# First half of the first norm's row spread over the partitions by TensorE, with identity products before and after it

## The chip, the cores and the metric

The kernel runs on one core of a Trainium2 chip. The metric is the device time of one execution in microseconds (us), taken as the median of several runs. Each profile shown here belongs to one execution, which has its own time. Times in the views count from the start of the profiled span.

Engines are named as in the profile: PE is the matrix engine (TensorE), PEld its weight load, DVE the vector engine, ACT the scalar engine, POOL the general engine (GpSimd), SP the engine that here does nothing but issue transfers (DMAs).

## The reference

One layer of a hybrid decoder block on 512 tokens of width 2048. What the change touches is only the very first step: the norm of the input and the projection behind it.

```python
def rmsnorm(x, g):
    xf = x.astype(jnp.float32)
    y = xf * lax.rsqrt(jnp.mean(xf * xf, axis=-1, keepdims=True) + EPS)
    return (y * g.astype(jnp.float32)).astype(x.dtype)
...
h = rmsnorm(x, attn_pre_norm[l])
m = token_mixer(h, w_in[l], ...)
x = x + rmsnorm(m, attn_post_norm[l])
h = rmsnorm(x, ffn_pre_norm[l])
f = conv_ffn(h, w_ffn_in[l], conv_w[l], conv_b[l], w_ffn_out[l])
x = x + rmsnorm(f, ffn_post_norm[l])
```

The gain `g` of the first norm, `attn_pre_norm`, is a row of 2048 numbers. Every token, that is every partition of a tile, needs the same row.

## The kernel before

Tokens stand in four tiles of 128 (t = 0 to 3), the width in 16 slots of 128. All matrix products are made in three passes: each float32 operand is split into a high part, rounded by ACT (`act(hi, raw, AF.Copy)`, L122, or L135 for activations), and a low remainder by DVE (`tt(lo, raw, hi, subtract)`, L123, or L136). PE then multiplies hi by hi, hi by lo and lo by hi (L176 to L178, L158 to L160, and later in the program L909 to L911 and L1006 to L1008). A weight block of 512 KB (`raw`, four buffers) becomes one pair `whi`, `wlo`.

`first_half` opens the program. It normalizes the tokens and makes the first half of one projection while the data still arrives. For each token tile t:

- `load_x(t)` fetches the tile in two transfers of 512 KB each (`xt`), and `load_w` fetches weight blocks.
- `bcast_row` fetches half of the gain row with one transfer that writes the same 4 KB to all 128 partitions of `gb` (512 KB written). The first half of the row is fetched right behind tile 0, the second at the end.
- `square(t)` sums squares on ACT (L231, in two halves), POOL forms the inverse root (L233, L129, L131: the tile `rs`).
- `scale(t, i)` multiplies on DVE by `rs` and by quarter i of `gb` (L238, 128x512 each).
- `turn(t, i)` transposes four 128x128 blocks on PE against the identity `ident` (L143), and splits the result into `ah` (ACT, L135) and `al` (DVE, L136).
- `prods(t, g)` makes the six products of token tile t with weight block g (L176 to L178).

The order in which PE, ACT, DVE and POOL run the steps of `first_half` is the order in which the code is written. SP isn't among these engines: where its transfers stand in its queue is chosen by the scheduler, from a simulated time line. The same scheduler orders all engines in the rest of the program. All transfers of SP use eight completion counters in turn (`DMAHW0` to `DMAHW7`), so SP issues a transfer only when the one issued eight places before it has landed. That makes SP's queue readable: when a transfer is issued late, the one eight places ahead has just landed.

Far behind, at the end of the feed-forward part, `down_unit` (L1006 to L1008) starts when the pool `ff` takes over the memory of an earlier pool. Every fourth weight block there is split into `xhi`, `xlo` of that pool in place of `whi`, `wlo`.

`bank()` gives a PSUM bank from a ring of four (pool `psa`), `qk_tile` a 128x512 tile from a ring of six.

Of the kernel before, what the change touches and what calls it, by code (L numbers as in the profile page):

```python
# [9 lines left out]
F32 = mybir.dt.float32  # L10
# [7 lines left out]
P = 128  # L18
# [17 lines left out]
def hybrid_layer(ctx: ExitStack, tc: tile.TileContext, x, attn_pre_norm, w_in, w_alpha_up, b_alpha,  # L36
# [3 lines left out]
    nc = tc.nc  # L40
# [6 lines left out]
    def dma(o, i):  # L47
        return nc.sync.dma_start(out=o, in_=i)
# [7 lines left out]
    mm = nc.tensor.matmul  # L56
# [3 lines left out]
    few = ctx.enter_context(tc.tile_pool(name="few", bufs=1, side="right"))  # L60
# [4 lines left out]
    ident = few.tile([P, P], F32, name="ident")  # L65
# [11 lines left out]
    def bank(pool=None):  # L77
        return (pool or psa).tile([P, 512], F32, name="bank", tag="bank")
# [21 lines left out]
    def load(src, a):  # L100
        raw = wpool.tile([P, GR], F32, name="raw", tag="raw", bufs=4)
        dma(raw.rearrange("p (a b) -> p a b", a=a), src)
        return raw
# [8 lines left out]
    def granule(src, a, raw=None, spare=None, bufs=4, hl=None):  # L112
        if raw is None:
            raw = load(src, a)
        if hl is not None:
            hi, lo = hl[:, 0, :], hl[:, 1, :]
        elif spare:
            hi = spare.tile([P, GR], F32R, name="xhi", tag="xhi", bufs=bufs)
            lo = spare.tile([P, GR], F32R, name="xlo", tag="xlo", bufs=bufs)
        else:  # L120
            hi, lo = halves()
        act(hi, raw, AF.Copy)  # L122
        tt(lo, raw, hi.bitcast(F32), ALU.subtract)  # L123
        r = "p (a b) -> p a b"
        return hi.rearrange(r, a=a), lo.rearrange(r, a=a)

    def rsqrt_mean(ss, n, width=1):
        t = small.tile([P, width], F32, name="ms", tag="ms")
        nc.gpsimd.tensor_scalar(t, ss, 1.0 / n, EPS, ALU.mult, ALU.add)  # L129
        r = small.tile([P, width], F32, name="rs", tag="rs")  # L130
        nc.gpsimd.tensor_tensor(r, t, nhalf[:, :width], ALU.pow)  # L131
        return r
# [5 lines left out]
    def transpose_into_act(src, t, slot0, n):  # L138
        for g in range(0, n, 4):
            m = min(4, n - g)  # L140
            b = bank()
            for j in range(m):
                nc.tensor.transpose(b[:, j * P:(j + 1) * P], src[:, (g + j) * P:(g + j + 1) * P], ident)  # L143
            bv = b[:, :m * P].rearrange("p (k c) -> p k c", k=m)
            split(ah[:, t, slot0 + g:slot0 + g + m, :], al[:, t, slot0 + g:slot0 + g + m, :], bv)

    def bcast_row(tile_ap, row):
        dma(tile_ap, row.partition_broadcast(P))
# [23 lines left out]
    def mm_n(banks, t, g, w):  # L172
        for k in range(2):
            s = 2 * g + k
            st, sp = s == 0, s == KT - 1
            mm(banks[t], ah[:, t, s, :], w[0][:, k, :], start=st, stop=False)  # L176
            mm(banks[t], ah[:, t, s, :], w[1][:, k, :], start=False, stop=False)  # L177
            mm(banks[t], al[:, t, s, :], w[0][:, k, :], start=False, stop=sp)  # L178
# [17 lines left out]
    def big8(name):  # L196
        return mx.tile([P, 2048], F32, name=name, tag="big8", bufs=6)

    def qk_tile(name):
        return mx.tile([P, S], F32, name=name, tag="qk", bufs=6)  # L200
# [5 lines left out]
    def first_half(c):  # L206
        gb = big8("gb")
        jb = mx.tile([P, 1024], F32, name="jb", tag="jb", bufs=1)
        xts = [big8("xt") for _ in range(NT)]
        w3 = mx.tile([P, 2, GR], F32R, name="w3", tag="big8", bufs=6)  # L210
        H2 = [slice(1024 * i, 1024 * (i + 1)) for i in range(2)]
        H4 = [slice(512 * i, 512 * (i + 1)) for i in range(4)]
        rs, raws, w = {}, {}, {}
        banks = [bank(psm) for _ in range(NT)]
        col = C_GV + 512 * c

        def load_x(t):
            for i in range(2):
                dma(xts[t][:, H2[i]], x2[t * P:(t + 1) * P, H2[i]])

        def load_w(*gs):
            for g in gs:
                raws[g] = load(w_in3[:, 2 * g:2 * g + 2, col:col + 512], 2)

        def weights(g):
            w[g] = granule(None, 2, raws[g], hl=w3 if g == 3 else None)

        def square(t):
            ss = small.tile([P, 2], F32, name="ss2", tag="ss2", bufs=4)
            for i in range(2):  # L230
                act(jb, xts[t][:, H2[i]], AF.Square, accum_out=ss[:, i:i + 1])  # L231
            sm = small.tile([P, 1], F32, name="ss", tag="ss")
            nc.gpsimd.tensor_tensor(sm, ss[:, 0:1], ss[:, 1:2], ALU.add)  # L233
            rs[t] = rsqrt_mean(sm, D)

        def scale(t, *ps):
            for i in ps:
                stt(xts[t][:, H4[i]], xts[t][:, H4[i]], rs[t], gb[:, H4[i]], ALU.mult, ALU.mult)  # L238

        def turn(t, *ps):  # L240
            for i in ps:
                transpose_into_act(xts[t][:, H4[i]], t, 4 * i, 4)

        def prods(t, *gs):
            for g in gs:
                mm_n(banks, t, g, w[g])

        load_x(0)
        bcast_row(gb[:, H2[0]], attn_pre_norm[0, H2[0]])
        load_w(0, 1, 2)  # L250
        load_x(1)
        load_w(3)
        load_x(2)
        load_x(3)
        bcast_row(gb[:, H2[1]], attn_pre_norm[0, H2[1]])
        square(0)
        scale(0, 0, 1)
        weights(0)
        turn(0, 0, 1)
        weights(1)  # L260
        weights(2)
        square(1)
        prods(0, 0, 1)
        scale(1, 0, 1)
        prods(0, 2)
        weights(3)
        turn(1, 0, 1)
        square(2)
        prods(0, 3)
        square(3)  # L270
        scale(2, 0, 1)
        prods(1, 0, 1, 2)
        turn(2, 0, 1)
        prods(1, 3)
        scale(3, 0, 1)
        prods(2, 0, 1)
        turn(3, 0, 1)
        scale(0, 2, 3)
        prods(2, 2)
        turn(0, 2, 3)  # L280
        scale(1, 2, 3)
        prods(2, 3)
        turn(1, 2, 3)
        scale(2, 2, 3)
        prods(3, 0, 1)
        turn(2, 2, 3)
        scale(3, 2, 3)
        prods(3, 2)
        turn(3, 2, 3)
        prods(3, 3)  # L290
        return banks

    with tc.manual_schedule(engines=IN_ORDER):
        banks = first_half(0)
# [914 lines left out]
```

## Time and profile before

| | us |
|---|---|
| runs: median (lowest to highest of 3) | 2176.3 (2173.17 to 2177.24) |
| the profiled execution, its own time | 2167.47 |
| its span, first to last instruction | 2165.8 |
| PE busy in the span | 2127.6 |
| DVE, ACT, POOL busy | 1416.9, 900.0, 205.1 |
| mean granted TensorE clock | 0.996 of full speed |
| data moved | 303.83 MB, 140 GB/s on the mean |

A row of the time line gives start, duration, engine, line, operation and shapes, how many were merged, and in brackets how long the engine had been idle and what ended that. The chain of waits goes back from the end of a stretch: at each step to what released the work. A row of the stretches gives, for each engine, busy time and number of instructions, then the granted TensorE clock, the share of busy DMA engines and the rate in GB/s. A merged duration of matrix products overlaps: the step from one start to the next is the pace.

### The profile page before, as it was taken

What the parts mean: (1) busy time and instruction counts of PE and PEld (TensorE: products, weight loads), DVE (VectorE), ACT (ScalarE), POOL (GpSimd) and SP (SyncE); (2) the same over time, 40 slices, a digit from 0 to 9 for tenths busy, and PEclk for the clock granted to TensorE, in tenths of its full rate; (3) what the DMA queues carried; (4) which work ended last, traced back from release to release, by engine and by line L of the source; (5) the groups of instructions that cost most, each with busy time, mean ns of one, the idle gap of its engine ahead of it and who ended that gap; (6) DMA issues with size and microseconds to landing.
All of it is one profiled execution on the core that took longest, in us unless ns stands there. A gap on an engine that the chain in (4) does not pass through costs nothing.

```text
span 2165.8 us, 31887 instructions
## 1 busy us (share of the span) xinstructions
PE 2127.6 (98%) x13009; PEld 1895.7 (88%) x13009; DVE 1416.9 (65%) x1722; ACT 900.0 (42%) x1162; POOL 205.1 (9%) x245
## 2 busy tenths in 40 slices
PE   7999999999999999999999999999999899999997
PEld 6878888888888889899999999999999778888886
DVE  5345553444444236787777686787877777888987
ACT  4233332333333234344444543544444465443533
POOL 1000000000000000011101111111111011011101
PEclk9999999999999999999999999999999999999999
DMA  6322222222224334355666757667577578677663
GB/s 212 104 69 78 79 75 81 70 78 86 78 88 166 100 133 174 128 127 140 159 160 160 158 141 180 157 139 188 142 169 180 163 218 214 179 191 180 160 171 136
DMA packets 218471, 303.83 MB, mean 140 GB/s; under 512 B 11776, under 2 KB 155572, under 8 KB 216404
## 3 DMA queue, kind: packets, MB, share of 16 engines
q1 hardware_dynamic: 165204, 238.87, 32.9%
q0 software_dynamic: 53120, 62.92, 18.9%
q8 instruction: 102, 1.67, 0.3%
q14 instruction: 45, 0.37, 0.0%
HBM read 273.97 MB, written 27.79 MB: 139 GB/s over the span
## 4 chain that ended last, share of the span: by engine, by line
issue 46%; PE 45%; POOL 4%; DVE 2%; DMA 1%; ACT 1%; POOLq 0%; SPq 0%; DVEq 0%; ACTq 0%
PE bank L177 6%; PE bank L176 6%; PE bank L178 6%; PE bank L160 5%; PE bank L158 5%; PE bank L159 5%; PE bank L1007 2%; PE bank L1008 2%; PE bank L1006 2%; POOL rt L858 2%; POOL raw L858 2%; PE bank L426 1%; PE bank L494 1%; PE bank L525 1%; PE bank L143 1%
## 5 line engine op out<-in xcount | busy, mean ns | idle before, releaser
L123 DVE TENSOR_TENSOR wlo<-raw,whi 128x1024 fp32r<-128x1024 f32 x307 | 374.2, 1222 | 361.6 <-ACT whi L122 353.5
L122 ACT ACTIVATE whi<-raw 128x1024 fp32r<-128x1024 f32 x307 | 324.8, 1059 | 599.7 <-PE bank L178 158.0
L911 PE MATMUL bank<-ah,wlo 128*128 128x256 f32 x1280 | 358.1, 280 | 0.9 <-DVE wlo L123 0.9
L909 PE MATMUL bank<-ah,whi 128*128 128x256 f32 x1280 | 357.9, 280 | 0.1
L910 PE MATMUL bank<-al,whi 128*128 128x256 f32 x1280 | 357.8, 280 | 0.0
L123 DVE TENSOR_TENSOR wlo<-rt,whi 128x1024 fp32r<-128x1024 f32 x220 | 267.7, 1221 | 95.1 <-ACT whi L122 93.0
L122 ACT ACTIVATE whi<-rt 128x1024 fp32r<-128x1024 f32 x220 | 232.1, 1059 | 231.2 <-PE bank L910 169.6
L910 PEld LDWEIGHTS bank<-al,whi 128*128 128x128 f32 x1280 | 244.0, 191 | 0.1
L911 PEld LDWEIGHTS bank<-ah,wlo 128*128 128x128 f32 x1280 | 240.2, 188 | 1.4 <-DVE wlo L123 1.3
L909 PEld LDWEIGHTS bank<-ah,whi 128*128 128x128 f32 x1280 | 240.3, 188 | 0.4 <-ACT whi L122 0.3
L176 PE MATMUL bank<-whi,ah 128*128 128x512 f32 x600 | 236.6, 397 | 0.4 <-ACT ah L135 0.4
L177 PE MATMUL bank<-wlo,ah 128*128 128x512 f32 x600 | 235.6, 393 | 0.0
L178 PE MATMUL bank<-whi,al 128*128 128x512 f32 x600 | 234.9, 393 | 0.0
L158 PE MATMUL bank<-ah,whi 128*128 128x512 f32 (+1 forms) x512 | 196.0, 383 | 0.0
L160 PE MATMUL bank<-ah,wlo 128*128 128x512 f32 (+1 forms) x512 | 194.6, 380 | 0.0
L159 PE MATMUL bank<-al,whi 128*128 128x512 f32 (+1 forms) x512 | 194.4, 380 | 0.0
L1007 PE MATMUL bank<-wlo,ah 128*128 128x512 f32 x420 | 163.7, 390 | 2.4 <-DVE wlo L123 2.4
L1008 PE MATMUL bank<-whi,al 128*128 128x512 f32 x420 | 163.3, 389 | 0.0
L1006 PE MATMUL bank<-whi,ah 128*128 128x512 f32 x420 | 155.9, 390 | 0.2 <-DVE acc L1014 0.2
L178 PEld LDWEIGHTS bank<-whi,al 128*128 128x128 f32 x600 | 113.1, 188 | 24.0 <-DVE al L136 0.3
L176 PEld LDWEIGHTS bank<-whi,ah 128*128 128x128 f32 x600 | 113.1, 189 | 23.8 <-ACT ah L135 0.8
L177 PEld LDWEIGHTS bank<-wlo,ah 128*128 128x128 f32 x600 | 113.1, 189 | 23.7 <-DVE wlo L123 0.5
(259 smaller groups left out, 4084.1 us busy)
## 6 DMA issues: line engine op xcount, KB each, us to landing
raw<-in_w_in_dram SPq DMA_DIRECT2D x96, 512.0 KB, 3.7
raw<-in_w_ffn_in_dram SPq DMA_DIRECT2D x96, 512.0 KB, 4.7
raw<-in_w_ffn_out_dram SPq DMA_DIRECT2D x48, 512.0 KB, 6.3
rt<-in_w_ffn_in_dram SPq DMA_DIRECT2D x40, 512.0 KB, 5.9
rt<-in_w_ffn_in_dram POOLq DMA_DIRECT2D x40, 512.0 KB, 6.1
raw<-in_w_ffn_in_dram POOLq DMA_DIRECT2D x40, 512.0 KB, 7.4
raw<-in_w_o_dram SPq DMA_DIRECT2D x32, 512.0 KB, 3.7
rt<-in_w_ffn_out_dram SPq DMA_DIRECT2D x20, 512.0 KB, 7.7
```

The source lines that it names most:

```text
L122: act(hi, raw, AF.Copy)
L123: tt(lo, raw, hi.bitcast(F32), ALU.subtract)
L158: mm(o, wh, ah[:, t0:t1, kk, :], start=st, stop=False)
L159: mm(o, wh, al[:, t0:t1, kk, :], start=False, stop=False)
L160: mm(o, wl, ah[:, t0:t1, kk, :], start=False, stop=sp)
L176: mm(banks[t], ah[:, t, s, :], w[0][:, k, :], start=st, stop=False)
L177: mm(banks[t], ah[:, t, s, :], w[1][:, k, :], start=False, stop=False)
L178: mm(banks[t], al[:, t, s, :], w[0][:, k, :], start=False, stop=sp)
L909: mm(o, wh, sh[:, :, kk, :], start=start and kk == 0 and n == 0, stop=False, **NOW)
L910: mm(o, wh, sl[:, :, kk, :], start=False, stop=False, **NOW)
L911: mm(o, wl, sh[:, :, kk, :], start=False, stop=kk == HK - 1, **NOW)
L1007: mm(b[j], sh[:, o:o + P], w[1][:, q, :], start=False, stop=False, **NOW)
```

## The change

```diff
+        row = qk_tile("row"), qk_tile("row")
+        for i in range(2):
+            dma(row[i][0:1, :], attn_pre_norm[0:1, H4[i]])
+        ones = few.tile([1, P], F32, name="ones")
+        nc.vector.memset(ones, 1.0)
         load_x(0)
-        bcast_row(gb[:, H2[0]], attn_pre_norm[0, H2[0]])
         load_w(0, 1, 2)
+
+        def idle_products(n):
+            scratch = bank()
+            for i in range(n):
+                mm(scratch[:, :P], ident, ident, start=True, stop=True)
+
+        idle_products(3)
+        for i in range(2):
+            g = bank()
+            mm(g, ones, row[i][0:1, :], start=True, stop=True)
+            nc.vector.tensor_copy(gb[:, H4[i]], g)
+        idle_products(6)
         load_x(1)
         load_w(3)
         load_x(2)
```

The first half of the gain row is no longer written to 128 partitions by one transfer. Two transfers of 2 KB bring it to one partition, as two quarters. PE multiplies a column of 128 ones by each quarter, which puts the quarter into all 128 rows of a PSUM bank, and DVE copies the bank to `gb`. Three products of the identity with itself stand ahead of these two products on PE, six behind them; nothing reads their result. The second half of the row still comes by its broadcast transfer.

The new steps take four banks of the ring of four and two tiles of the ring of six. Lines behind the change stand 18 lines further down.

On PE, at the start of the program, the rows are these now (the transposes of L143 stood first before). A name in brackets is a counter of the engine that is waited for.

```order
L261 MATMUL bank<-ident 128x128 [waits Pool_49]
L261 MATMUL bank<-ident 128x128 x2
L266 MATMUL bank<-row,ones 128x512 [waits DMAHW0_49,DVE_49]
L266 MATMUL bank<-row,ones 128x512 [waits DMAHW1_49]
L261 MATMUL bank<-ident 128x128 x6
L143 MATMUL bank<-ident,xt 128x128 [waits DMAHW2_49,DVE_49,PE_49]
```

Eleven products stand ahead of the first transpose, the first of them behind POOL, which makes the identity, and the row's two behind their transfers.

SP's queue at the start of the program, before (the rows of `xt` come in the order of the tiles, two for each):

```order
L48 DMA xt<-in_x_dram 128x1024 x2
L48 DMA gb<-in_attn_pre_norm_dram 128x1024
L48 DMA raw<-in_w_in_dram 128x2x512 x3
L48 DMA xt<-in_x_dram 128x1024 x2
L48 DMA raw<-in_w_in_dram 128x2x512 [waits DMAHW0_49]
L48 DMA xt<-in_x_dram 128x1024 [waits DMAHW1_49]
L48 DMA xt<-in_x_dram 128x1024 [waits DMAHW2_49]
L48 DMA xt<-in_x_dram 128x1024 [waits DMAHW3_49]
L48 DMA xt<-in_x_dram 128x1024 [waits DMAHW4_49]
L48 DMA gb<-in_attn_pre_norm_dram 128x1024 [waits DMAHW5_49]
L48 DMA gnb<-in_gla_norm_dram 128x256 [waits DMAHW6_49]
L48 DMA dnb<-in_diff_norm_dram 128x256 [waits DMAHW7_49]
```

And now:

```order
L48 DMA row<-in_attn_pre_norm_dram 1x512 x2
L48 DMA xt<-in_x_dram 128x1024 x2
L48 DMA raw<-in_w_in_dram 128x2x512 x4
L48 DMA gb<-in_attn_pre_norm_dram 128x1024 [waits DMAHW0_49]
L48 DMA gnb<-in_gla_norm_dram 128x256 [waits DMAHW1_49]
L48 DMA xt<-in_x_dram 128x1024 [waits DMAHW2_49]
L48 DMA xt<-in_x_dram 128x1024 [waits DMAHW3_49]
L48 DMA xt<-in_x_dram 128x1024 [waits DMAHW4_49]
L48 DMA xt<-in_x_dram 128x1024 [waits DMAHW5_49]
L48 DMA xt<-in_x_dram 128x1024 [waits DMAHW6_49]
L48 DMA xt<-in_x_dram 128x1024 [waits DMAHW7_49]
L48 DMA dnb<-in_diff_norm_dram 128x256 [waits DMAHW0_49]
```

More has moved than the diff says. The fourth weight block, the second half of the gain row and the row `gnb`, which stood behind tile 1, now stand ahead of it. Before, tile 1 stood behind tile 0, one broadcast and three weight blocks.

One place on PE differs far from the change, in `down_unit`, where the scheduler has drawn another order (the rest of PE's program reads alike). Before:

```order
L1006 MATMUL bank<-whi,ah 128x512 x2
L1007 MATMUL bank<-wlo,ah 128x512
L1008 MATMUL bank<-whi,al 128x512
L1006 MATMUL bank<-whi,ah 128x512
L1007 MATMUL bank<-wlo,ah 128x512
L1008 MATMUL bank<-whi,al 128x512
L1007 MATMUL bank<-wlo,ah 128x512
L1008 MATMUL bank<-whi,al 128x512
L1006 MATMUL bank<-whi,ah 128x512
L1007 MATMUL bank<-wlo,ah 128x512
L1008 MATMUL bank<-whi,al 128x512
L1006 MATMUL bank<-xhi,ah 128x512 x2
```

And now (L1024 to L1026 are L1006 to L1008 of before):

```order
L1025 MATMUL bank<-wlo,ah 128x512
L1026 MATMUL bank<-whi,al 128x512
L1024 MATMUL bank<-whi,ah 128x512
L1025 MATMUL bank<-wlo,ah 128x512
L1026 MATMUL bank<-whi,al 128x512
L1025 MATMUL bank<-wlo,ah 128x512
L1026 MATMUL bank<-whi,al 128x512
L1024 MATMUL bank<-whi,ah 128x512
L1025 MATMUL bank<-wlo,ah 128x512
L1026 MATMUL bank<-whi,al 128x512
L1024 MATMUL bank<-xhi,ah 128x512 x2
L1024 MATMUL bank<-whi,ah 128x512
```

The two products that led the group now stand behind the two that read `xhi`.

## Prediction

> **What bounds the kernel now.** First the page's head, then the waits of PE over the whole span.
>
> ```profile
> span 2165.8 us, 31887 instructions
> PE 2127.6 (98%) x13009; PEld 1895.7 (88%) x13009; DVE 1416.9 (65%) x1722; ACT 900.0 (42%) x1162; POOL 205.1 (9%) x245
> ```
> ```profile
> PE bank L143 <- DVE xt L238: 10.4, 2, 9.5
> PE bank L1006 <- ACT xhi L122: 8.7, 2, 7.4
> ```
>
> PE is without work for only 2165.8 - 2127.6 = 38.2 us. One gap of 9.5 us lies at the start, where the change is, one of 7.4 us far behind. So PE sets the end, and whatever moves its start moves the end, unless a later wait takes it up. The later waits end when ACT or DVE have worked on what PE itself delivered, or when a transfer lands whose buffer PE's own progress freed, so they move along with PE. I pass a shift at the start through one to one.
>
> Next the chain of waits over the first 26 us: what released what until PE ran on without a break.
>
> ```profile
> 4.30 11.02 DMA xt<-in_x_dram
> ...
> 15.40 1.16 ACT jb L231 x2
> ...
> 17.18 0.57 POOL rs L131
> ...
> 18.45 0.74 DVE xt L238
> 19.19 1.15 DVE w L123
> ...
> 20.38 0.50 PE bank L177
> 20.88 0.23 PE bank L178
> ```
>
> This decides the case. The chain doesn't go through tile 0 and its gain row at all. It goes through the transfer of tile 1's second half, issued at 4.30 and waited for until 15.40, then its squares, its inverse root, its scaling, the split of weight block 3, and PE at 20.38. From there PE runs at a pace of 0.23 us. The time line of the transfer queue shows why tile 1 is late.
>
> ```profile
> 0.80 0.86 SPq L48 DMA_DIRECT2D xt<-in_x_dram  x2
> 1.71 0.42 SPq L48 DMA_DIRECT2D gb<-in_attn_pre_norm_dram  x1
> ...
> 3.78 0.99 SPq L48 DMA_DIRECT2D xt<-in_x_dram  x2
> ...
> 14.05 0.33 SPq L48 DMA_DIRECT2D gnb<-in_gla_norm_dram  x1
> 15.33 0.33 SPq L48 DMA_DIRECT2D dnb<-in_diff_norm_dram  x1
> ```
>
> `gnb` and `dnb` wait for the transfers eight places ahead, which are the halves of tile 1: they landed at about 14.05 and 15.33, behind all that was issued before them.
>
> **The change part by part.** First tile 0. Its steps on ACT, POOL, DVE and PE, from the time line:
>
> ```profile
> 5.66 1.06 ACT L231 ACTIVATE jb<-xt 128x1024 f32<-128x1024 f32 x1 [0.38 <-DMA xt<-in_x_dram]
> ...
> 7.45 0.56 POOL L131 TENSOR_TENSOR rs<-ms,nhalf 128x1 f32<-128x1 f32 x1
> 8.69 1.41 DVE L238 SCALAR_TENSOR_TENSOR xt<-xt,rs,gb 128x512 f32<-128x512 f32 x2 [7.03 <-DMA gb<-in_attn_pre_norm_dram]
> 9.50 1.97 PE L143 MATMUL bank<-ident,xt 128*128 128x128 f32 x8 [9.50 <-DVE xt L238]
> ...
> 17.78 1.41 DVE L238 SCALAR_TENSOR_TENSOR xt<-xt,rs,gb 128x512 f32<-128x512 f32 x2 [1.71 <-POOL rs L131]
> ```
>
> The removed broadcast held the scaling until 8.69. The inverse root was ready at 7.45 + 0.56 = 8.01, and for tile 1 DVE starts 0.04 behind it (17.18 + 0.57 = 17.75, 17.78), so without the broadcast 8.05 would do: 0.64 us to be had. Against it stand the two row transfers, issued ahead of tile 0. Two issues take 0.86 us, with the gap 0.9, so tile 0 is issued 0.9 us later and its root comes at up to 8.9. Its second half no longer shares the queue with the broadcast, which gives a little back. I take 8.9 for the scaling, 0.2 later than now (bounds 8.4 and 9.1).
>
> The new work on PE and DVE has to fit ahead of that. The identity's last step, and a plain float32 product of 512 columns for the price:
>
> ```profile
> 1.57 0.28 POOL masks.py:199 TENSOR_SCALAR_AFFINE_SELECT ident<-ident 128x128 f32<-128x128 f32 x1
> ```
> ```profile
> L382 PE MATMUL bank<-gaT,wup 80*128 80x512 f32 x8 | 3.8, 592 | 0.0
> ```
>
> PE can begin at 1.85. A 128x128 float32 product at the start costs 1.97 / 8 = 0.25 us by the eight transposes, so three cost 0.75 and six 1.5. A 512-column one costs 0.59 us at full pace, about 1.1 at the start's pace (the ratio of 0.43 to 0.23, below). Rows of 2 KB should land well before the 4.1 us at which the first 512 KB of tile 0 had. Taking 3.0: products until 5.2, the two copies on DVE (at most the 0.7 us of a scaling each) until 5.9, the six identity products until 6.7. Even with rows as late as 5.66 all is over by 9.4, while the transposes then start at 9.7. So I cost all eleven products and both copies at nothing; the wait for tile 0 hides them. Were it gone, they would cost up to 0.75 + 2.2 + 1.5 = 4.5 us.
>
> Now the term that counts, tile 1. Ahead of and with its second half, the queue moved eight transfers of 512 KB. Now it moves nine and `gnb` with 128 KB, since weight block 3, the second broadcast and `gnb` have been drawn ahead. The rates, from the stretches of the start:
>
> ```profile
> 3.00:4.50 1.50, 0.00 (x0) 0.00 (x0) 0.00 (x0) 0.37 (x1) 0.00 (x0) 1.00 0.89 309
> 4.50:6.00 1.50, 0.00 (x0) 0.00 (x0) 0.00 (x0) 1.12 (x3) 0.00 (x0) 1.00 1.00 259
> 6.00:8.00 2.00, 0.00 (x0) 0.00 (x0) 0.00 (x0) 0.81 (x2) 0.94 (x3) 1.00 0.99 261
> ...
> 9.00:12.00 3.00, 2.09 (x9) 1.69 (x9) 2.22 (x4) 1.72 (x3) 0.00 (x0) 1.00 1.05 412
> ```
>
> 640 KB more at 412 GB/s is 0.655 / 0.412 = 1.6 us. The later issue adds 0.9. On the other side, from 4.5 to 8, when the removed broadcast was under way, the queue moved only 260 GB/s at full business: 3.5 x (1 - 260 / 412) = 1.3 us lost, which may go away with it. Upper end: the broadcast that now stands in the way is as slow in its new place, 1.6 + 0.9 = +2.5. Lower end: the slowness goes, and the rows use time in which nothing moved anyway, 1.6 - 1.3 = +0.3. I take the later issue whole, since the queue is empty until then, and most of the relief: 1.6 + 0.9 - 1.1 = **+1.4 us**. It passes whole along the chain above: behind 15.40 every step waits for the one before. Weight block 3 comes earlier now, but its split stands behind tile 1's scaling on DVE.
>
> Last, the other place on PE. There the time line has:
>
> ```profile
> 1755.06 1.06 ACT L122 ACTIVATE xhi<-raw 128x1024 fp32r<-128x1024 f32 x1 [7.26 <-DMA raw<-in_w_ffn_out_dram]
> ...
> 1756.16 0.73 PE L1006 MATMUL bank<-xhi,ah 128*128 128x512 f32 x2 [1.31 <-ACT xhi L122]
> ```
>
> PE already waits 1.31 us for `xhi` here. Two products that ran ahead of the wait now run behind it, so it grows by 2 x 0.23 = 0.45 us if the transfer lands when it did, by nothing if it moves. I take **+0.2**.
>
> Sum: 1.4 + 0.2 = **+1.6 us**; tile 0's 0.2 vanishes behind tile 1. For the profiled execution (span 2165.8, 2167.47 with what lies around it) that gives 2169.1. The median of the runs stands 8.8 us above that execution; nothing in the change bears on that distance, so I forecast 2176.3 + 1.6 = **2177.9**.
>
> **The rivals.** First the clock, which could make it slower. Two starts, and stretches at the start and around the late gap:
>
> ```profile
> 15.13 0.63 PE L176 MATMUL bank<-whi,ah 128*128 128x512 f32 x1
> ...
> 15.56 0.63 PE L177 MATMUL bank<-wlo,ah 128*128 128x512 f32 x1
> ```
> ```profile
> 9.50:12.90 3.40, 2.99 (x10) 1.00 1.05 416
> 12.90:16.30 3.40, 3.40 (x8) 1.00 1.01 394
> ```
> ```profile
> 1729.80:1733.30 3.50, 0.04 (x1) 0.04 (x1) 0.06 (x1) 2.03 (x3) 0.00 (x0) 0.50 0.36 146
> 1733.30:1736.60 3.30, 3.26 (x7) 2.16 (x8) 2.39 (x2) 0.78 (x1) 0.00 (x0) 0.50 0.97 397
> ```
>
> From its first work at 9.50 to about 16.3 PE steps by 0.43 us, then by 0.23 (the granted clock of 1.00 in these rows isn't recorded for the start). After 12.9 it had no gap, from 9.5 to 12.9 only 2.99 of 3.40 were busy. In the late gap the clock reads 0.50, and stays so for 3.3 us after work returns. If now PE does tile 0's products in pieces and waits for tile 1 at about 20, the slow pace can reach beyond that wait. Each slow microsecond there loses 1 - 0.23 / 0.43 = 0.47 us. A stretch of 3.4 us loses 1.6, one as long as the first (6.8) loses 3.2: in all +3.2 to +4.8, **2180.3**. For it: three weight splits on DVE still break up tile 0's products. Against it: at the slow pace those 18 products alone fill 7.7 us nearly without a gap. It leaves no-change from a slow stretch of 5.9 us on.
>
> Second, faster: the new products bring PE to its fast pace before tile 0, and tile 1 isn't late, because transfers overlap more than I count. Eight transposes take 1.03 us at the fast pace:
>
> ```profile
> 25.73 1.03 PE L143 MATMUL bank<-ident,xt 128*128 128x128 f32 x8
> ```
>
> Then tile 0's transposes give 1.97 - 1.03 = 0.94 and the wait for the broadcast 0.64, less the 0.9 of the later issue: -0.7, with the other place -0.5, **2175.8**. For it: about 4.5 us of products stand where PE was idle. Against it: tile 1's second half would have to land at 14.6, with 640 KB more ahead of it. The most that a fast start could ever give is 6.8 x 0.47 + 0.64 = 3.8 us, below what can be told from no change.
>
> The Trainium skill, "TensorE: Matmul & The Clock Gate", section "What's actually happening", has the clock rise after about 3.4 us of sustained work and fall after one idle window of that length, with windows that run freely. By that rule the new products may lift it before tile 0, and a wait below 3.4 us mostly wouldn't drop it, which speaks for the second rival's pace and against the first. The trace agrees in the gap at 1726 to 1733, where the clock halves and comes back in steps of this size; that 2.99 busy of 3.40 didn't lift it says that small holes count.
>
> That the products don't fill the wait for tile 0 (they end near 6.7 by my sum, PE then idles 3 us) is a way in which the change wouldn't do what it says; it gives the forecast's time, as tile 1 decides.
>
> **How the numbers follow.** Forecast 0.55, slow clock 0.25, faster start 0.14, something else 0.06 (the gap of 7.4 us with its slow stretch may fall differently). The runs shown lie within 2173.17 to 2177.24, so about 0.2%, or 4.35 us, is what a measurement can tell from no change. Slower by more (above 2180.65): 0.07 from the forecast with its upper end, 0.14 from the clock, 0.03 from the rest, 0.24. Faster by more (below 2171.95): only by scatter, 0.07. Within: 0.69. The forecast's own range is 2176.6 to 2179.3 by the bounds of its terms (+0.3 to 2.5 + 0.45); with the rivals and the scatter of 2 us the range is 2173.5 to 2182.0.
>
> **What would show it.** Right: tile 1's second half lands at 16 to 17.5; ACT waits for it ahead of the second squares; PE stands idle ahead of tile 1's transposes for 1 us or more, and the unbroken run starts near 21.8. The identity products end before tile 0's scaling. Wrong: tile 1 lands by 15.3, or the pace after its transposes is 0.43, or a new wait of PE appears behind 25 us that the profile of before doesn't have.

## The result and the profile after

The change made the kernel slower, and the time lies outside the predicted range.

| | before | after |
|---|---|---|
| runs: median (lowest to highest of 5 each) | 2176.3 (2173.17 to 2182.4) | 2184.02 (2182.74 to 2185.03) |
| ratio, 95% interval | | 1.0031 (1.0016 to 1.0046) |
| profiled execution, its own time | 2167.47 | 2185.03 |
| its span | 2165.8 | 2183.3 |
| PE busy in the span | 2127.6 | 2147.7 |

The two profiled executions differ by 17.6 us, the medians by 7.7. The difference in PE's busy time, 20.1 us, is larger still although the change adds only eleven products (8.4 us by the rows below). Most of what is left over has another cause than the start, which the experiments brought out (below); the start is read first. The page's head and PE's waits of after:

```profile
span 2183.3 us, 31937 instructions
PE 2147.7 (98%) x13031; PEld 1910.3 (87%) x13031; DVE 1419.8 (65%) x1725; ACT 900.4 (41%) x1162; POOL 205.0 (9%) x245
```
```profile
PE bank L1024 <- ACT xhi L122: 8.1, 3, 7.3
PE bank L143 <- DVE xt L238: 3.9, 1, 3.9
...
PE bank L261 <- POOL ident masks.py:199: 1.9, 1, 1.9
```

The wait of 9.5 us ahead of tile 0's transposes is gone, since the new products fill it:

```profile
1.91 1.65 PE L261 MATMUL bank<-ident 128*128 128x128 f32 x6 [1.91 <-POOL ident masks.py:199]
...
3.49 3.78 PE L266 MATMUL bank<-row,ones 1*128 1x512 f32 x4
...
7.20 2.93 PE L261 MATMUL bank<-ident 128*128 128x128 f32 x12
```

Each of these products is recorded as two passes (x6 for three products, x4 for two, x12 for six). A wait of 3.9 us ahead of tile 1's transposes has come. The chain of waits over the first 28 us of after (start, duration, what):

```profile
6.30 11.85 DMA xt<-in_x_dram
...
18.23 1.16 ACT jb L231 x2
...
20.02 0.57 POOL rs L131
...
20.61 0.77 DVE xt L238
...
21.42 1.97 PE bank L143 x8
23.38 0.43 PE bank L176
...
26.79 0.31 PE bank L178
27.10 0.23 PE bank L176
```

The same chain as before decides: tile 1's second half, squares, root, scaling, and now the transposes where the split of weight block 3 came last before. Two things are new in it. The half is waited for until 18.15, and its squares start at 18.23, not 15.40. And behind the transposes PE steps by 0.43 us until 26.8. Stretches of after (PE's busy time first, the granted clock third from the end):

```profile
2.00:8.00 6.00, 6.00 (x13) 3.23 (x14) 1.38 (x2) 2.37 (x5) 0.74 (x3) 1.00 0.91 291
8.00:18.20 10.20, 9.04 (x36) 7.09 (x35) 6.64 (x8) 5.29 (x7) 0.64 (x2) 1.00 1.01 369
...
18.00:21.00 3.00, 0.00 (x0) 0.00 (x0) 0.39 (x1) 2.24 (x5) 0.94 (x3) 0.83 1.03 423
...
20.00:24.00 4.00, 2.58 (x10) 2.42 (x11) 3.24 (x4) 1.50 (x4) 0.56 (x1) 0.50 0.88 240
24.00:27.00 3.00, 3.00 (x9) 2.33 (x8) 0.89 (x2) 2.94 (x6) 0.52 (x3) 0.53 1.06 235
```

and of before for the same work, up to tile 1's second squares:

```profile
2.00:8.00 6.00, 0.00 (x0) 0.00 (x0) 0.00 (x0) 2.37 (x5) 1.37 (x4) 1.00 0.96 288
8.00:15.40 7.40, 5.49 (x15) 3.90 (x16) 5.92 (x8) 4.98 (x7) 0.01 (x1) 1.00 1.03 403
```

By the time tile 1's second half was there, after had moved 6 x 291 + 10.2 x 369 = 5.51 MB, before 6 x 288 + 7.4 x 403 = 4.71 MB. The 0.80 MB more are 2.0 us at 403 GB/s. The lower rate makes up the rest: 10.2 x (1 - 369 / 403) = 0.9 us. Together that is 2.9, against 18.23 - 15.40 = 2.8 seen; the sum says where the time lies and not why. Most of the lower rate lies in one stretch (2 x (1 - 251 / 403) = 0.75 us), in which the second half of the gain row and `gnb` were landing (at 14.44 and 15.67, by the transfers issued behind them). The first row is after, the second h1, another execution of the same kernel, in which that dip is missing:

```profile
12.00:14.00 2.00, 2.00 (x7) 1.34 (x6) 1.63 (x3) 2.00 (x3) 0.00 (x0) 1.00 0.94 251
12.00:14.00 2.00, 1.54 (x7) 0.86 (x5) 2.00 (x4) 1.99 (x3) 0.00 (x0) 1.00 1.03 396
```

Then the clock: from 20 to 27 us it stood at about 0.5 in after (a mean of 0.83 from 18 to 21 is 1.00 until 20.0 and 0.50 behind). It had come up sooner than before, whose pace was 0.43 us until 16.3:

```profile
13.11 0.43 PE L176 MATMUL bank<-whi,ah 128*128 128x512 f32 x1
13.38 0.39 PE L177 MATMUL bank<-wlo,ah 128*128 128x512 f32 x1
13.60 0.39 PE L178 MATMUL bank<-whi,al 128*128 128x512 f32 x1
...
17.15 0.39 PE L178 MATMUL bank<-whi,al 128*128 128x512 f32 x1
```

So PE was done with tile 0 at 17.5, and then had nothing until 21.42.

How late the start leaves PE can be read further on, where nothing of it changes any more: the first long row of PE in the chain behind 170 us starts at 171.25 in before and at 175.90 in after.

```profile
171.25 1.73 PE bank L426 x16
```
```profile
175.90 1.73 PE bank L444 x16
```

The start therefore costs 4.65 us. Both rows are used below as a marker; in other kernels the line's number differs by a few.

### The profile page after: what moved, and what is told of

The parts are those of the page before. It is cut to its first block, busy times and chain, and to the rows that moved or that the text cites. A ratio compares the mean times of both kernels' runs of the same rounds, so it can differ in the third digit from the quotient of the medians.

```text
span 2183.3 us, 31937 instructions
## 1 busy us (share of the span) xinstructions
PE 2147.7 (98%) x13031; PEld 1910.3 (87%) x13031; DVE 1419.8 (65%) x1725; ACT 900.4 (41%) x1162; POOL 205.0 (9%) x245
## 4 chain that ended last, share of the span: by engine, by line
PE 75%; issue 19%; DVE 2%; POOL 2%; DMA 1%; ACT 1%; POOLq 0%; SPq 0%; DVEq 0%; ACTq 0%
PE bank L929 10%; PE bank L927 10%; PE bank L928 10%; PE bank L176 6%; PE bank L177 6%; PE bank L178 6%; PE bank L160 5%; PE bank L158 5%; PE bank L159 5%; PE bank L444 1%; PE bank L1025 1%; PE bank L1026 1%; PE bank L1024 1%; POOL rt L876 1%; PE bank L512 1%
## 5 line engine op out<-in xcount | busy, mean ns | idle before, releaser
L1026 PE MATMUL bank<-whi,al 128*128 128x512 f32 x420 | 163.4, 389 | 0.0
L1024 PE MATMUL bank<-whi,ah 128*128 128x512 f32 x420 | 157.2, 392 | 1.5 <-ACT whi L122 1.1
```

## The experiments

Each time stands beside that of before, measured next to it on the same chip. The marker is the row near 171 us of the one profiled execution. The intervals of e4, f4, g1 and h1 all reach one, so that the argument on the start goes by the markers and the rows behind them, and the medians only agree with its direction.

| run | median (lowest to highest, runs) | before beside it | ratio, 95% interval | marker |
|---|---|---|---|---|
| e1 before again | 2177.63 (2173.28 to 2180.58, 12) | 2176.55 | 1.0001 (0.9992 to 1.0011) | 171.36 |
| e2 loads first | 2176.26 (2169.85 to 2180.39, 12) | 2176.55 | 1.0005 (0.9991 to 1.0019) | 170.80 |
| e3 no identity products | 2148.25 (2147.08 to 2151.64, 4) | 2176.55 | 0.9874 (0.9856 to 0.9893) | 171.13 |
| e4 before, tile 1 late | 2179.52 (2168.39 to 2184.48, 12) | 2176.55 | 1.0014 (0.9999 to 1.0030) | 174.08 |
| f1 two banks | 2177.84 (2168.25 to 2182.12, 10) | 2176.82 | 1.0003 (0.9991 to 1.0016) | 172.74 |
| f2 four banks | 2176.64 (2171.28 to 2180.27, 10) | 2176.82 | 0.9996 (0.9985 to 1.0007) | 171.16 |
| f3 before, two banks | 2176.07 (2158.97 to 2178.58, 10) | 2176.82 | 0.9984 (0.9960 to 1.0007) | 171.43 |
| f4 filler, 32 products | 2179.79 (2167.20 to 2183.41, 10) | 2176.82 | 1.0005 (0.9990 to 1.0019) | 176.41 |
| g1 filler, 16 products | 2179.29 (2176.84 to 2182.62, 10) | 2176.58 | 1.0012 (0.9998 to 1.0026) | 173.54 |
| g2 one standstill | 2166.55 (2159.21 to 2183.23, 10) | 2176.58 | 0.9971 (0.9942 to 0.9999) | |
| g3 ten standstills | 2207.95 (2203.81 to 2208.61, 4) | 2176.58 | 1.0148 (1.0116 to 1.0180) | |
| h1 after again | 2180.66 (2164.86 to 2186.06, 12) | 2177.14 | 1.0015 (0.9996 to 1.0033) | 175.00 |
| h2 e3 again | 2176.19 (2160.80 to 2179.00, 12) | 2177.56 | 0.9982 (0.9964 to 1.0000) | 171.08 |

### Is it the order of SP's queue? (e1, e2, e4)

e1 is before without an edit.

> The kernel before, unchanged. In the profiled execution of before, PE stepped by 0.113 us in place of 0.118 from about 1370 to 1570 us, which the changed kernel's execution did not show. If that is a matter of the single execution, this profile should lack it somewhere else or altogether, have a span near 2174, and the ratio to the runs of before is 1.000 within 0.002. If it belongs to the kernel, the span is again near 2166 and the stretch is there again.

e2 keeps every piece of the change and moves only tile 1's transfers ahead of the code of the identity products, so that SP's queue serves tile 1 first as before:

```diff
         load_w(0, 1, 2)
+        load_x(1)
+        load_w(3)
+        load_x(2)
+        load_x(3)
+        bcast_row(gb[:, H2[1]], attn_pre_norm[0, H2[1]])
...
         idle_products(6)
-        load_x(1)
-        load_w(3)
-        load_x(2)
-        load_x(3)
-        bcast_row(gb[:, H2[1]], attn_pre_norm[0, H2[1]])
```

> The changed kernel with the same products, but with the loads written ahead of them; only SP's queue differs, and has tile 1 ahead of weight block 3, the second half of the gain row and gnb, as before. Theory (tile 1's late transfer carries the loss at the start): tile 1's second half lands near 15, its transposes start near 18.3 in place of 21.4, the clock doesn't fall, and 3 to 5 us of the changed kernel's loss are gone (2179 to 2181, or as fast as before). Rival (the products on PE or the copies on DVE cost the time): the start stays as late as in the changed kernel, about 4.6 us behind before, and the time stays near 2184.

e4 is the other way round: before, with weight block 3 and the second broadcast ahead of tile 1 and nothing else of the change but the order of PE in `down_unit`, which follows by itself:

```diff
-        load_w(0, 1, 2)
+        load_w(0, 1, 2, 3)
+        bcast_row(gb[:, H2[1]], attn_pre_norm[0, H2[1]])
         load_x(1)
-        load_w(3)
         load_x(2)
         load_x(3)
-        bcast_row(gb[:, H2[1]], attn_pre_norm[0, H2[1]])
```

> The kernel before with weight block 3 and the second half of the gain row loaded ahead of tile 1, and nothing else changed at the start: broadcast by transfer, no new products. 1 MB more stands ahead of tile 1 than before. Theory (queue order alone makes the loss): tile 1's second half lands near 17.5, the start is 2 to 5 us later than before, the time near 2179. Rival (the new products make it): within 1 us of before.

The time line of e2, squares of tile 1's second half, scaling, transposes:

```profile
14.96 1.06 ACT L231 ACTIVATE jb<-xt 128x1024 f32<-128x1024 f32 x1
17.33 1.41 DVE L238 SCALAR_TENSOR_TENSOR xt<-xt,rs,gb 128x512 f32<-128x512 f32 x2 [2.00 <-POOL rs L131]
...
18.14 1.38 PE L143 MATMUL bank<-ident,xt 128*128 128x128 f32 x8 [1.08 <-DVE xt L238]
```

and the same of e4, with its clock behind:

```profile
18.19 1.06 ACT L231 ACTIVATE jb<-xt 128x1024 f32<-128x1024 f32 x1
20.56 1.41 DVE L238 SCALAR_TENSOR_TENSOR xt<-xt,rs,gb 128x512 f32<-128x512 f32 x2 [4.25 <-POOL rs L131]
...
21.37 1.32 PE L143 MATMUL bank<-ident,xt 128*128 128x128 f32 x8 [1.70 <-DVE xt L238]
```
```profile
20.00:24.00 4.00, 2.38 (x13) 1.70 (x14) 3.44 (x5) 2.17 (x4) 0.53 (x1) 1.00 0.88 243
```

With all identity products, row products and copies in place, but tile 1 first, the squares start at 14.96, ahead of before's 15.40, and the marker stands 0.45 us ahead of before's. So those pieces, written in this order, cost nothing. With none of them, but tile 1 behind two transfers more, the squares start at 18.19 and the marker is 174.08 - 171.25 = 2.8 us late; 1.0 MB more at 403 GB/s are 2.6. So the queue's order alone can make tile 1 as late as in after. It isn't the same sum: e4 has two transfers of 512 KB more ahead of tile 1, after one and `gnb`. f4 and g1 (below) have after's queue and squares at 17.47 and 17.65, h1 at 18.49, so that this order is worth 2.1 to 3.1 us by the execution. But e4's marker stands 1.8 us ahead of after's at equal lateness of tile 1 (18.19 and 18.23): its clock stays at 1.00, and eight transposes take 1.32 us, not 1.97. The rest of after's loss is the clock.

### Is the rest the clock? (f4, g1)

In after PE finishes tile 0's products at 17.5 and stands still until 21.42. f4 puts 32 identity products into that hole (`idle_products(8)` four times), g1 puts 16, which is the edit shown:

```diff
         weights(3)
+        for _ in range(4):
+            idle_products(4)
         turn(1, 0, 1)
```

> The changed kernel with 32 more identity products on TensorE ahead of tile 1's transposes, eight in each of four banks, so that the ring of four stands as after. Theory of the clock (after loses about 1.5 us because TensorE is idle from 17.4 to 21.4 us and its clock drops from 19.93 to 26.76): no drop at 19.93, the first product of tile 1's weights about 3 us later than before and not 3.2, and the lag at 27 us about 2.9 to 3.2 us where after has 4.4 to 4.6; total 1 to 2 us below after, about 2182.5. Rival (the drop has another cause): lag 4.4 to 4.6 us as after, or more by what the added products take.

f4 overfilled the hole. The clock stayed at 1.00, but the time line shows the added passes (two for each product) until 24.65, with tile 1's transposes at 24.49 queued behind them:

```profile
17.35 7.30 PE L261 MATMUL bank<-ident 128*128 128x128 f32 x64
...
24.49 1.04 PE L143 MATMUL bank<-ident,xt 128*128 128x128 f32 x8
```

Tile 1 was scaled from 19.84, so the transposes could have begun about 3.8 us earlier, and the marker shows the opposite of what was hoped (176.41). Half the dose:

> The changed kernel with 16 identity products on TensorE ahead of tile 1's transposes, four in each of four banks: half as many as in f4, whose 64 passes ran from 17.35 to 24.65 us and so held up the transposes, which could have started at about 21.3. Theory of the clock: the 32 passes end near 21.0, the clock stays at 1.00, tile 1's transposes start near 21.4 at the full clock, and against before the lag at 27 us is 2.3 to 3.1 us where after has 4.4 to 4.6; total about 2182 us in an execution at the slow pace of 0.1178 us throughout. Rival (the clock drops for want of something else than products on TensorE): the drop at about 20 us is there as after, lag 4.4 to 4.6 us.

```profile
17.31 3.73 PE L261 MATMUL bank<-ident 128*128 128x128 f32 x32
...
20.88 1.33 PE L143 MATMUL bank<-ident,xt 128*128 128x128 f32 x8
```
```profile
20.00:24.00 4.00, 3.74 (x25) 3.00 (x24) 3.95 (x6) 2.32 (x5) 0.00 (x0) 1.00 1.06 254
24.00:27.00 3.00, 3.00 (x15) 2.49 (x14) 0.71 (x2) 2.94 (x5) 0.94 (x3) 1.00 0.77 229
```

The clock stays at 1.00 through the stretch where after has 0.50, and the marker comes at 173.54, 2.4 us ahead of after's. Of these, 0.6 come from tile 1, which in this execution was scaled at 20.02 and not at 20.61; the other 1.8 us are what the slow stretch cost. The rival, by which the clock drops for want of something else than products on PE, falls.

### Where do 28 us come and go? (e3, f1, f2, f3, g2, g3, h2)

e3 is the changed kernel without the nine identity products (the scheduler then keeps tile 1 first in SP's queue by itself):

```diff
-        idle_products(3)
         for i in range(2):
             g = bank()
             mm(g, ones, row[i][0:1, :], start=True, stop=True)
             nc.vector.tensor_copy(gb[:, H4[i]], g)
-        idle_products(6)
```

> The changed kernel without the nine identity products. The scheduler then leaves tile 1 in its old place in SP's queue. Theory (queue order): the loss at the start goes as in the kernel with the loads first, within 1 us of it, since PE's early work isn't on the path; PE steps by 0.43 us until about 16. Rival (identity products are worth something by the clock): slower than the kernel with the loads first by 1 to 3 us.

Its start was as fast as before's (marker 171.13), and then it came out 28 us ahead, in all four runs. The stretches of the up-projection show where. e1 (before again), a stage far behind the change:

```profile
950.00:1100.00 150.00, 150.00 (x1276) 150.00 (x1275) 111.46 (x113) 70.47 (x77) 17.95 (x14) 1.00 0.65 155
1375.00:1580.00 205.00, 205.00 (x1743) 205.00 (x1742) 153.99 (x157) 93.10 (x101) 28.25 (x22) 1.00 0.65 155
```

and e3:

```profile
950.00:1100.00 150.00, 150.00 (x1326) 150.00 (x1325) 116.28 (x119) 72.81 (x80) 20.53 (x16) 1.00 0.67 160
1375.00:1580.00 205.00, 205.00 (x1810) 205.00 (x1809) 157.60 (x161) 97.63 (x107) 28.25 (x22) 1.00 0.71 169
```

PE is busy throughout and the clock is 1.00 in both, but 1276 products of 128x256 are made in 150 us in the one, 1326 in the other: 0.118 and 0.113 us each. Nothing lies between: steps from start to start are 0.117 to 0.119 in the one pace and 0.113 to 0.114 in the other. At some 750 us the faster pace is worth 750 x (1 - 0.1133 / 0.1178) = 29 us. The profiled execution of before had it for a part, from about 1355 to 1586 us:

```profile
1130.00:1340.00 210.00, 210.00 (x1785) 210.00 (x1784) 158.98 (x162) 96.28 (x104) 26.97 (x21) 1.00 0.63 149
1375.00:1580.00 205.00, 204.67 (x1804) 204.28 (x1803) 158.44 (x162) 94.38 (x102) 28.30 (x22) 1.00 0.70 163
```

The changed kernel's profiled execution had the slower pace throughout, and so the two differ by far more than the change. Followed product by product, after lags before by 4.65 us from 60 to 780 us, by 5.55 from 801 to 1350, by 12.0 at 1600 and by 17.6 at the end. The pace, with some late products of before among it, makes 6.5 of that, the last stage 5.6; there e1, the same program as before, also loses 4.3 us to it. Since PE counts as busy all through the stage, its busy time carries the pace as well. The step from one to the other shows in e3 as one product whose successor starts 0.15 us behind it; shortly after it the pace is the faster one:

```profile
941.59 0.32 PE L927 MATMUL bank<-s2h,wlo 128*128 128x256 f32 x1
941.74 0.28 PE L925 MATMUL bank<-s2h,whi 128*128 128x256 f32 x1
```

The first theory was that the place in the ring of PSUM banks sets the pace: e3 takes two banks at the start, where before takes none and after four. f1 is e2 with all nine identity products in the bank of the first row product, f2 is e3 with two single identity products in banks of their own, f3 is before with two such products:

```diff
         load_w(0, 1, 2)
+        for _ in range(2):
+            scratch = bank()
+            mm(scratch[:, :P], ident, ident, start=True, stop=True)
```

> The changed kernel with tile 1 loaded first as in e2, and with all nine identity products put into the bank of the first row product, so that the start takes two banks of the ring of four and not four. Theory of the banks (the pace of the up-projection hangs on where the ring stands: two banks at the start put it on the fast pace): about 2148 us, 0.1133 us a product from about 942 us on, as in e3. Rival of the count (the nine products themselves, by number or time, keep the slow pace): about 2176 us, 0.1178 us a product throughout.

> e3 with two single identity products, each in a bank of its own at the two places where after has three and six, so that the start takes four banks again; nothing else differs from e3 on any engine. Theory of the banks: back to about 2176 us and 0.1178 us a product. Rival of the count: two products of about 0.25 us that lie behind the wait for the first tile change nothing, 2148 us and 0.1133 us a product as in e3.

> The kernel before with two single identity products ahead of the first transposes, each in a bank of its own, and nothing else. Theory of the banks: the ring stands as in e3, so about 2148 us and 0.1133 us a product from about 942 us on. Rival (it is something else of e3, the row by TensorE among it): 2174 to 2180 us, the slow pace.

f1 and f3 have e3's place in the ring and are not faster than before. The theory of the banks falls. f2 came out as that theory said, but so did everything else. The rival of f1 and f2, that the number of products matters, was no better off: f2 differs from e3 by two products, each of two passes and some 0.5 us. The profiled execution of f1 was at the slower pace until a product came some 0.2 us late at 1119 us, and at the faster one from then on. Its start was 1.5 us slower than before's. The rows show why: its nine identity products stand ahead of the row's two, whose copies start at 8.16 and 9.87; so tile 0 is scaled at 10.48, not at 8.71 as in e2, and tile 1's second squares start at 16.84, not at 14.96. The new products cost nothing only where the row's two come early. Since the faster pace came behind a late product in e3 and in f1, a standstill was tried: one identity product that must wait for a copy of what PE has just written, in the second unit of the up-projection of before (g2) or in every second one (g3):

```diff
-        u.y0()
+        if i == 1:
+            with tc.manual_schedule(engines={ET.PE}):
+                turnback = few.tile([P, P], F32, name="turnback", bufs=1)
+                act(turnback, u.banks["z"][:, :P], AF.Copy)
+                s = bank()
+                mm(s[:, :P], ident, turnback, start=True, stop=True)
+                bank()
+                u.y0()
+        else:
+            u.y0()
```

> The kernel before, with one identity product in the second unit of the up-projection (at about 945 us) that has to wait for a copy by ScalarE of what TensorE has just written, so that TensorE stands still once for 1 to 2 us. Theory (the pace of 0.1133 us a product is a state that TensorE enters behind a short standstill and then keeps): 0.1133 us from there to about 1700 us, total about 2150 us. Rival (a standstill does not set the pace): 0.1178 us as mostly before, total 2177 to 2179 us.

> As g2, with such a standstill in every second unit of the up-projection instead of in one. Theory (each standstill offers the fast pace again): about ten standstills cost 10 to 20 us, and the pace is 0.1133 us in most units; total 2155 to 2170 us. Rival: 0.1178 us in all units, total 2187 to 2197 us.

g2's stretches show the faster pace soon behind the standstill, lost again at about 1369 us, at another late product, and found again at 1584:

```profile
990.00:1340.00 350.00, 350.00 (x3091) 350.00 (x3090) 268.88 (x274) 165.23 (x179) 46.94 (x37) 1.00 0.69 163
1375.00:1580.00 205.00, 205.00 (x1743) 205.00 (x1742) 150.94 (x153) 90.95 (x98) 25.80 (x21) 1.00 0.70 165
```

Its median is 10 us below before's, where the theory wanted 27. So a standstill may bring the faster pace, and it doesn't hold it. g3 had the faster pace almost throughout, and paid more than it won, 2208 us, more than both theories allowed. One reason is the waits themselves, which were longer than the 1 to 2 us intended:

```profile
PE bank L1048 <- ACT turnback L1046: 37.2, 10, 5.0
```

That is 3.7 us each (2.64 us in g2). The other is the clock, whose mean over g3's span was 0.989 against 0.996: it fell to half behind eight of the ten, for 3.4 or 6.8 us, 34 us in all, of which 16 us are lost by the ratio of the two paces at the start (1 - 0.23 / 0.43 = 0.47). With 29 us won, if the faster pace had held throughout, that makes 24 of the 31 us measured; the rest is open. In g2 the faster pace likewise came just as such a slow stretch ended, from 983 to 986 us, so there the standstill and the step of the clock aren't told apart. In e3 and f1 there was no step of the clock. g2's standstill:

```profile
982.04 0.49 PE L1048 MATMUL bank<-turnback,ident 128*128 128x128 f32 x2 [2.64 <-ACT turnback L1046]
```

That left e3 itself. It was run again, with more executions:

> e3 once more (the changed kernel without the nine identity products). Theory of the kernel (something in its order of work leads to a short standstill at 941.8 us in every execution, behind which the pace of 0.1133 us a product is kept): 2147 to 2152 us in all runs again. Rival of chance (the pace is drawn anew in each execution, and e3's four runs all happened to draw it): a spread from about 2150 to 2180 us, median above 2165 us.

2176.19 us, from 2160.80 to 2179.00, its profiled execution at 0.1178 us a product throughout. So e3's gain doesn't belong to the kernel: the same program gave 2148 in four runs and 2176 in twelve. Nor does it look like a draw made anew in each execution, since none of the twelve came below 2160.80 and all four below 2152; the four were taken together on another chip, and what they had in common isn't told apart here. **No version found beats before**; e3 does not, and g2 gains 0.3% with an interval that nearly reaches one. What draws the pace stays open.

### What does the change cost beyond the start? (h1)

> The changed kernel once more, for what is left of its loss beyond the start (7.7 us between the medians, of which the start shows 4.4 to 4.6). Theory of the start (the rest is the 0.95 us at 792 us and chance in the last stage, where executions of one kernel differ by some us, and in the pace of the up-projection): median 2180.5 to 2182.5 us over ten or more runs, some of them at or below 2179, the lag at 27 us again 4.4 to 4.6. Rival (the change costs a further 3 us later on as well, every time): median 2183.5 to 2184.5 us, all runs within 1.5 us, as in the first five.

Twelve further runs have a median of 2180.66 beside 2177.14 for before, 3.5 us more, and the lowest, 2164.86, shows that after can be quick too. The five runs of the first measurement were all on the high side; a further cost of 3 us each time is ruled out. A small one remains in both executions of after, 0.9 us at about 804 us, where PE waits 0.77 us for `xlo` and before 0.29. It isn't shown to be the change's: g2, whose start is before's, waits 0.8 us there, and g1 not at all. The marker expected (lag of 4.4 to 4.6) was missed: 175.00, a lag of 3.75. Its clock shows why:

```profile
20.00:24.00 4.00, 2.33 (x10) 2.23 (x11) 3.10 (x4) 1.51 (x3) 0.74 (x2) 0.63 0.80 212
24.00:27.00 3.00, 3.00 (x14) 2.42 (x13) 1.03 (x3) 2.94 (x6) 0.35 (x2) 0.92 0.90 226
```

Tile 1 was scaled even later (20.86 instead of 20.61), but the clock was down for some 3.4 us only, not for 6.8.

## Why the prediction was wrong, step by step

- **What bounds the kernel**: right. The chain through tile 1's second half decides, and a shift at the start reaches the marker whole (2.8 us at the squares of e4, 2.8 at its marker), and after's lag of 4.65 us still stands at 780 us.
- **Tile 0, the eleven products and the copies at nothing**: right, but with less room than I gave. After scales tile 0 at 8.76 (8.69 before, 8.9 forecast); e2, which has all of it, is not slower than before. I priced each product as one pass, 4.5 us in all; each is two, and they took 1.65 + 3.78 + 2.93 = 8.4 us. So the last ended at about 10 and not at 6.7, and held tile 0's transposes up by 0.4 us (9.92 for 9.50), off the path. In f1, where nine of them stand ahead of the row's two, the start is 1.5 us slower.
- **Tile 1's second half, +1.4 us: this is the step that failed.** It was 2.8 us late in after and 3.1 in h1, beyond my upper bound of 2.5, and 2.1 and 2.25 in f4 and g1, whose queue is the same. Its direction, place and passing on were right; it was mis-sized. I had 1.6 for the bytes, 0.9 for the later issue and 1.1 back from the removed broadcast. In after the bytes cost 2.0, the later issue and the relief cancelled (both kernels moved 1.7 MB from 2 to 8 us), and the rate fell from 403 to 369 GB/s behind, 0.9 us, most of it in the dip in which the rows drawn ahead were landing. In h1 that dip is missing, and instead only 256 GB/s moved from 2 to 8 us, where before has 288; why either comes stays open. The relief was the part taken too large. In e2, e3, f1 and h2, which have no first broadcast and the old order, `dnb` is issued, and so tile 1's second half has landed, at 13.9 to 14.9, 0.5 to 1.4 us ahead of before. One transfer less (1.3 us) and the later issue (0.7 measured: tile 0's second squares at 6.38, not at 5.66) alone give 0.6, so the relief is worth up to 0.8 us and not 1.1.
- **The clock, a rival at a chance of 0.25: it came true on top of the forecast**, through a door that I had not seen. I argued that the first slow pace might last beyond the wait. In fact the new products lifted the pace sooner (0.23 us from 13.1 on, before from 16.3), so that PE was done with tile 0 at 17.5; with tile 1 2.8 us late, it then stood still for 3.9 us, and in that time the clock fell to 0.50. In g1 the filled hole saves 1.8 us of 4.65. I had argued that a wait below 3.4 us mostly wouldn't drop the clock. The runs bear that out only in part: 1.70 us in e4 did not drop it, 3.88 in after did, but so did a standstill of 2.64 us in g2, behind which the clock was at 0.50 from 983 to 986 us. In after it fell at about 20.0, when PE had been idle for 2.4 us. So the rule cited from the Trainium skill ("TensorE: Matmul & The Clock Gate", "What's actually happening"), by which the clock falls after one idle window of about 3.4 us, is not met to the letter in these two places: less than 3.4 us of idleness was enough. Small holes don't always keep the clock down either: in h1 it came back at about 24.5, though PE was busy for only 2.8 of the 3.4 us before.
- **The other place, +0.2**: its wait for `xhi` is 7.3 us at the longest as before (7.4); the total of such waits moved from 8.7 to 8.1. Nothing to be seen.
- **The sum and its base**: the start costs 4.65 us in the profiled execution (3.75 in h1), where I had 1.4: 2.8 for the half and 1.8 for the clock, which the sum had at nothing. I put the 8.8 us between the profiled execution of before and the median aside as unexplained. e1's execution of the same program, 10.9 us longer, shows what they hold: 6.5 us of faster pace and 4.3 in the last stage. On 2176.3 the start's 4.65 would give 2181, still inside the range; that the first five runs lay 3 us higher looks like chance, since h1's twelve lie 3.5 us above before. That the forecast was too low is not chance.
- **The signs named beforehand**: ACT waits ahead of the squares of tile 1 (2.64 us), PE idles more than 1 us ahead of its transposes (3.88), no new wait of weight behind 25 us: as forecast. The half landed at about 18.2, outside the 16 to 17.5; the identity products ended behind tile 0's scaling; the slow steps after the transposes, named as a sign that I was wrong, were there.

## What to carry to other kernels

A transfer that decides the start is sensitive to code that doesn't touch it: here nine products whose result nobody reads, written ahead of the loads, went with a queue that has 512 KB and `gnb` more ahead of tile 1 (without them, e3, or with them behind the loads, e2, tile 1 stays first), and behind the loads the same products cost nothing. After any edit near the start, read the queue that issues the transfers first. And before a profiled execution is used as a base, count products per time in a long, fully busy stretch; if that differs between executions of one kernel, differences of the same size between two kernels say nothing without many runs, even where four runs agree within some 0.2%.

## What the runs showed of the hardware

- One stream of 128x256 products, with the same granted clock of 1.00 and no idle time, ran at either 0.1133 or 0.1178 us a product for hundreds of microseconds, and changed between the two mostly at a late product or a short standstill. It is worth up to 29 us of 2176. Four runs of one program all fell on the fast side and twelve later ones, on another chip, did not.
- The clock's record moves in lengths of about 3.4 us: down for some 6.8 us in after, 3.4 in h1, 3.4 or 6.8 behind eight of the ten standstills of g3 and not at all behind the other two. Idle times of 3.9 and 4.3 us at the same place cost 6.8 and 3.4 us of slow clock, and 2.64 us in g2 was enough for a drop.
- Identity products as filler keep the clock up (g1). Too many of them delayed the work that they were to speed up (f4): the transposes, ready at about 20.7, started behind the last of them at 24.49.
